# A list scheduler's later landings, its margin at projection matmuls and its cost of wide GpSimd additions, in a one-core encoder trunk

## Chip, cores and metric

The kernel runs on one core of one Trainium2 chip. The metric is the device time of one execution in microseconds; lower is better. Five engines work beside each other, each through its own instructions in a fixed order: TensorE (PE, with its weight loads shown as PEld), VectorE (DVE), ScalarE (ACT), GpSimd (POOL) and SyncE (SP), which issues the DMA transfers. An instruction that waits for a semaphore holds up all that stand behind it on its engine.

## The reference

One layer of an encoder trunk on 2048 prompt tokens and 32 sample tokens, model width 1024, all in float32. Each stream goes through a mixer and a feed-forward part, both with a shift, scale and gate that come from a conditioning vector:

```
p = h @ w_in                                   # 1024 -> 3080 columns
uv, qkv, z, ab = p[..., :o1], p[..., o1:o2], p[..., o2:o3], p[..., o3:]
a_out = spatial_gating(u, v, sgu_w, sgu_b)     # u, v = split(gelu(uv)), chunks of 128 positions
qkv, new_buf = causal_conv(qkv, conv_buf, conv_w)
o, s_new = gated_delta_rule(q, k, vv, beta, g, s0)   # 4 heads x 128, a state carried from chunk to chunk
out = jnp.concatenate([a_out, b_out], axis=-1) @ w_out
x = x + gt1 * m
h = rmsnorm(x, norm_ffn_g[l]) * (1 + sc2) + sh2
x = x + gt2 * (jnp.square(jax.nn.relu(h @ w_up[l])) @ w_down[l])   # 1024 -> 4096 -> 1024
```

A final RMSNorm follows. The outputs are the tokens of both streams and the states.

## The kernel before

Activations lie transposed, channels on the 128 partitions and tokens in the columns. Every large product is made of three matmuls on split operands: a value is cast to a rounded high part (on ACT), and the rest is the low part (a subtraction on DVE, in some places on POOL), and the product is high x high + low x high + high x low (`mm3`, and `split`, `operand`, `slab` for the operands). So each weight block that is loaded (in pieces of 256 or 512 KB) passes through ACT and then DVE before PE may use it.

The work comes in three stages. After a short start, `mixers` goes over two halves of the tokens: the projections of `w_in` column by column (`gemm`, in PSUM banks called g), the delta rule of four heads (`delta_local` and `delta_inv` within chunks, `delta_chain` over the chunks, in banks L, B and C), the spatial gating, and then the output projection. The delta chain hands a small product from PE to DVE or ACT and back several times a chunk; projection matmuls fill the time between. Last comes `feed_forward`, in four blocks of 520 tokens: `ffn_up` and `ffn_down` form their products from seven instead of eight block products each (sums and differences of the weights' and values' blocks), in single PSUM banks f that are taken and given back. In the first block the weights' sums are formed on POOL and stored for later blocks; later blocks load them again (`su_d`, `sd_d`). In `ffn_up`, bank X takes a product, DVE adds it to another value (`u2`, `v5`), and the bank then accumulates a further product, which therefore waits until DVE has read the bank.

The order of all this is not written by hand. Each operation is recorded with its engine, a cost in nanoseconds, what it reads and writes, and a priority: CHAIN, INV, LOCAL, EVAC, GEMM from first to last; the projections' matmuls alone have GEMM (`at(GEMM)` around `mm3`), and among those and the evacuations the one that is due first goes first. `Program.schedule` (L237) then plays the five engines and one DMA engine forward in time by those costs: an operation is ready when all before it have ended, plus a table's latency between the two engines (`LATENCY`), and each engine takes the ready operation of the first priority. A load occupies the planned DMA engine for its bytes / 360 ns, at least 500, and lands `DMA_LATENCY` later (a little sooner for small ones). The outcome is only an order for each engine; at run time the semaphores decide when each instruction starts. A planned time that is too short thus puts an instruction too early in its engine's line, and one that is too long puts it too late. `tt` (L343) sets the cost of an elementwise operation of two tensors; on POOL 150 ns and 2.1 ns a column, for narrow multiplications 1.65.

Of the kernel before, what the change touches and what calls it, by code (L numbers as in the profile page):

```python
# [11 lines left out]
ALU = mybir.AluOpType  # L12
# [28 lines left out]
PE, DVE, ACT, POOL, DMA, NONE = range(6)  # L41
TABLES = {AF.Silu: "silu", AF.Gelu_apprx_tanh: "gelu", AF.Exp: "exp", AF.Ln: "ln"}

DMA_LATENCY = 3000


LATENCY = {(PE, DVE): 230, (PE, ACT): 230, (PE, POOL): 230, (DVE, PE): 380, (DVE, DVE): 130, (DVE, ACT): 160,
           (DVE, POOL): 190, (DVE, DMA): 150, (ACT, PE): 370, (ACT, DVE): 175, (ACT, ACT): 180, (ACT, POOL): 210,
           (ACT, DMA): 150, (POOL, PE): 390, (POOL, DVE): 100, (POOL, ACT): 130, (POOL, POOL): 130, (POOL, DMA): 100}
# [5 lines left out]
CHAIN, INV, LOCAL, EVAC, GEMM, IDLE = range(6)  # L55
# [133 lines left out]
def R(x):  # L189
    return x.ap if isinstance(x, View) else x  # L190
# [10 lines left out]
class Program:  # L201
# [35 lines left out]
    def schedule(self):  # L237

        ops = self.ops
        due = [i if o.eng == PE and o.prio == GEMM else len(ops) for i, o in enumerate(ops)]  # L240
        for i in reversed(range(len(ops))):
            due[i] = min([due[i]] + [due[j] for j in ops[i].succ])
        key = [(o.prio, due[i] if o.prio >= EVAC else i, i) for i, o in enumerate(ops)]
        free = [0.0] * 6
        port = [0.0] * 6
        wait = [[] for _ in range(6)]
        ready = [([], []) for _ in range(6)]
        table, grid = None, (P, P)
        order = []

        def release(i, t):
            o = ops[i]
            if o.eng == NONE:
                finish(i, t, t)
            else:
                heapq.heappush(wait[o.eng], (t, i))

        def finish(i, start, end):
            o = ops[i]
            o.start = start  # L260
            order.append((start, i))
            for j in o.succ:
                s = ops[j]
                s.ready = max(s.ready, end + o.lat + LATENCY.get((o.eng, s.eng), 0.0))
                s.npred -= 1
                if s.npred == 0:
                    release(j, s.ready)

        for i, o in enumerate(ops):
            if o.npred == 0 and o.start == 0.0 and o.eng != NONE:  # L270
                heapq.heappush(wait[o.eng], (0.0, i))
        for i, o in enumerate(ops):
            if o.npred == 0 and o.eng == NONE and not any(k == i for _, k in order[-1:]):
                finish(i, 0.0, 0.0)
                o.npred = -1

        other = {DVE: POOL, POOL: DVE}
        while True:
            best = None
            for e in range(5):  # L280
                shared = port[other[e]] - PORT if e in other else 0.0
                t = None
                if ready[e][0]:
                    t = free[e]
                elif ready[e][1]:
                    t = max(free[e], shared)
                if wait[e]:
                    at, i = wait[e][0]
                    at = max(free[e], at, shared if ops[i].port else 0.0)
                    t = at if t is None else min(t, at)  # L290
                if t is not None and (best is None or t < best[0]):
                    best = (t, e)
            if best is None:
                break
            t, e = best
            while wait[e] and wait[e][0][0] <= t:
                i = heapq.heappop(wait[e])[1]
                heapq.heappush(ready[e][ops[i].port], key[i])
            shared = port[other[e]] - PORT if e in other else 0.0
            tops = [q for q in (ready[e][0], ready[e][1] if shared <= t else None) if q]  # L300
            if not tops:
                continue
            i = heapq.heappop(min(tops, key=lambda q: q[0]))[-1]
            o = ops[i]
            end = t + o.cost
            if e == PE:
                if o.table and o.table != grid:
                    end += 195 if o.table == (P, P) else 135
                    grid = o.table
            elif o.table and o.table != table:  # L310
                end += 1280
                table = o.table
            free[e] = end
            if o.port:
                port[e] = end
            finish(i, t, end)
        assert len(order) == len(ops), (len(order), len(ops))
        self.span = max(free)
        order.sort()
        return [ops[i] for _, i in order]  # L320


class Kern:
# [19 lines left out]
    def tt(self, out, a, b, op, eng=DVE):  # L343
        n = out.n
        if eng == DVE:
            c = 68 + 1.042 * n
        elif op == ALU.pow:
            c = 300 + 165 * n
        else:
            c = 150 + (1.65 if op == ALU.mult and n < 300 else 2.1) * n  # L350
        e = self._e(eng)
        self.p.op(eng, c, lambda: e.tensor_tensor(out=R(out), in0=R(a), in1=R(b), op=op), [out], [a, b])  # L352

# [31 lines left out]
    def dma(self, out, in_, n=None):  # L385
# [3 lines left out]
        x = b / 360  # L389
        self.p.op(DMA, max(500, x), lambda: nc.sync.dma_start(out=R(out), in_=R(in_)), [out], [in_], lat=DMA_LATENCY + min(0, x - 500))  # L390

# [1470 lines left out]
```

## Time and profile before

| what | value |
|---|---|
| time, median of 3 runs | 2437.33 us (2435.55 to 2437.97) |
| profiled execution, first to last instruction | 2450.8 us |
| mean granted clock of TensorE | 0.989 |
| DMA moved | 574.85 MB, 235 GB/s on average |

The runs are timed without the profiler, the profile is of one further execution; its span is 13.5 us above the median. No other time of the profiled execution is given. Busy times are read from the page's first part and from the busy times by stretch; "f<-s" is what an instruction writes and reads, by the program's names without buffer numbers, L398 the line of the matmul helper and L337, L352 and L357 those of ACT's and DVE's helpers, so groups are told apart by tiles and shapes. A bracket such as [2.02 <-DVE s L352] is the engine's idle time before an instruction and what ended it.

### The profile page before, as it was taken

The page shows a single profiled execution, that of the slowest core. Times are in us where ns is not written, and L with a number is a line of the kernel's source. Part 1 is how long each engine was busy: PE and PEld are TensorE (multiplying, and loading weights), DVE is VectorE, ACT ScalarE, POOL GpSimd, SP SyncE. Part 2 cuts the span into 40 slices and gives each one's busy share as a digit, 9 for nine tenths or more (in the row PEclk, how much of TensorE's full clock was granted, in tenths as well). Part 3 has the DMA queues.
Part 4 walks back from the last instruction along what each step waited for, and adds up shares of the span by engine and source line. Part 5 has one row for each costly group of instructions (what it writes and reads, how often), then busy time and mean ns, then how long its engine had stood idle before and what let it go on. Part 6 is the DMA issues. An engine that isn't in the chain of part 4 may idle for free.

```text
span 2450.8 us, 53625 instructions
## 1 busy us (share of the span) xinstructions
PE 2372.3 (97%) x18786; PEld 2217.0 (90%) x18786; DVE 1749.2 (71%) x4041; ACT 1563.5 (64%) x3727; POOL 790.0 (32%) x1079
## 2 busy tenths in 40 slices
PE   7998999999999999999999999999899999899998
PEld 4876878999999878999999999999899999899998
DVE  5555666556665546488677778889788888877786
ACT  4454656455565435375455687777788877887774
POOL 2134422202432223455333453333721213511111
PEclk9999999999999899999999999999999999999999
DMA  8688667555457767888667787888788877787773
GB/s 305 206 298 264 211 199 243 143 180 161 145 181 215 239 183 231 269 273 275 240 215 244 251 265 242 268 273 275 240 266 289 267 256 231 248 279 220 246 232 117
DMA packets 389687, 574.85 MB, mean 235 GB/s; under 512 B 71628, under 2 KB 201568, under 8 KB 389416
## 3 DMA queue, kind: packets, MB, share of 16 engines
q1 hardware_dynamic: 389416, 571.42, 72.2%
q8 instruction: 148, 2.42, 0.4%
q14 instruction: 123, 1.01, 0.1%
HBM read 434.80 MB, written 136.45 MB: 233 GB/s over the span
## 4 chain that ended last, share of the span: by engine, by line
PE 27%; DVE 9%; DMA 8%; ACT 5%; issue 2%; POOL 1%; SPq 0%; DVEq 0%; ACTq 0%; POOLq 0%
PE f L398 27%; DVE s L352 6%; DMA s<-su_d 3%; ACT s L337 2%; DVE s L357 1%; ACT wh L337 1%; DMA s<-w_u 1%; DMA wr<-su_d 1%; DVE wl L352 1%; DVE BL L352 1%; ACT wl L337 1%; DMA wr<-w_u 1%; POOL s L352 1%; DMA s<-sd_d 1%; DMA s<-th_d 0%
## 5 line engine op out<-in xcount | busy, mean ns | idle before, releaser
L337 ACT ACTIVATE s<-s 128x260 f32<-128x260 f32 (+11 forms) x1398 | 611.5, 464 | 338.8 <-DVE s L357 99.5
L398 PE MATMUL f<-s,s 128*128 128x260 f32 x3984 | 538.5, 284 | 8.2 <-ACT s L337 3.6
L352 POOL TENSOR_TENSOR s<-s,s 128x260 f32<-128x260 f32 (+3 forms) x369 | 374.3, 1027 | 518.1 <-ACT s L337 377.0
L398 PE MATMUL f<-BH,wh 128*128 128x260 f32 x1800 | 514.0, 286 | 13.4 <-DVE s L352 9.1
L398 PE MATMUL f<-BH,wl 128*128 128x260 f32 x1800 | 511.1, 284 | 3.6 <-DVE wl L352 2.6
L398 PEld LDWEIGHTS f<-s,s 128*128 128x128 f32 x3984 | 501.8, 189 | 13.6 <-DVE s L352 6.3
L398 PE MATMUL f<-BL,wh 128*128 128x260 f32 x1800 | 509.9, 283 | 1.9 <-DVE BL L352 1.9
L352 DVE TENSOR_TENSOR s<-s,s 128x260 fp32r<-128x260 f32 (+5 forms) x740 | 413.4, 576 | 71.3 <-ACT s L337 43.6
L398 PE MATMUL g<-BH,wh 128*128 128x512 f32 (+2 forms) x1112 | 424.7, 382 | 0.0
L352 DVE TENSOR_TENSOR s<-f,s 128x260 f32<-128x260 f32 x856 | 345.6, 420 | 94.6 <-PE f L398 91.4
L398 PE MATMUL g<-BH,wl 128*128 128x512 f32 (+2 forms) x1112 | 395.0, 355 | 0.0
L398 PE MATMUL g<-BL,wh 128*128 128x512 f32 (+2 forms) x1112 | 393.8, 354 | 0.6 <-DVE BL L352 0.6
L398 PEld LDWEIGHTS f<-BH,wh 128*128 128x128 f32 x1800 | 340.4, 189 | 18.1 <-DVE s L352 6.7
L398 PEld LDWEIGHTS f<-BH,wl 128*128 128x128 f32 x1800 | 341.0, 189 | 5.1 <-DVE wl L352 3.7
L398 PEld LDWEIGHTS f<-BL,wh 128*128 128x128 f32 x1800 | 341.1, 190 | 2.8 <-DVE BL L352 2.7
L352 POOL TENSOR_TENSOR s<-s 128x260 f32<-128x260 f32 (+11 forms) x321 | 167.3, 521 | 531.8 <-DVE s L352 264.1
L337 ACT ACTIVATE wh<-s 128x512 fp32r<-128x512 f32 (+1 forms) x364 | 228.0, 630 | 83.8 <-DMA s<-w_u 25.2
L398 PE MATMUL f<-BH,s 128*128 128x260 f32 x1040 | 240.0, 285 | 0.9 <-ACT BH L337 0.6
L398 PEld LDWEIGHTS g<-BH,wh 128*128 128x128 f32 x1112 | 212.4, 191 | 24.7 <-issue 8.5
L398 PEld LDWEIGHTS g<-BH,wl 128*128 128x128 f32 x1112 | 211.9, 191 | 19.6
L398 PEld LDWEIGHTS g<-BL,wh 128*128 128x128 f32 x1112 | 213.2, 192 | 15.2 <-DVE BL L352 1.1
L357 DVE SCALAR_TENSOR_TENSOR s<-s,s,s 128x512 f32<-128x512 f32 (+6 forms) x318 | 165.0, 535 | 70.5 <-ACT s L337 40.5
(119 smaller groups left out, 3566.4 us busy)
## 6 DMA issues: line engine op xcount, KB each, us to landing
s<-su_d SPq DMA_DIRECT2D x288, 256.0 KB, 4.2
s<-w_u SPq DMA_DIRECT2D x168, 256.0 KB, 4.1
s<-w_d SPq DMA_DIRECT2D x150, 256.0 KB, 4.5
s<-sd_d SPq DMA_DIRECT2D x115, 256.0 KB, 4.0
wr<-su_d SPq DMA_DIRECT2D x96, 256.0 KB, 3.9
wr<-w_b SPq DMA_DIRECT2D x42, 512.0 KB, 5.6
wr<-w_d SPq DMA_DIRECT2D x68, 256.0 KB, 4.7
s<-x_d SPq DMA_DIRECT2D x128, 130.0 KB, 3.6
```

Source lines behind the costliest of these rows:

```text
L337: self.p.op(ACT, c, lambda: nc.scalar.activation(out=R(out), in_=R(in_), func=func, **{k: R(v) for k, v in kw.items()}), [out, accum], [in ...
L352: self.p.op(eng, c, lambda: e.tensor_tensor(out=R(out), in0=R(a), in1=R(b), op=op), [out], [a, b])
L357: self.p.op(DVE, c, lambda: nc.vector.scalar_tensor_tensor(out=R(out), in0=R(a), scalar=R(s), in1=R(b), op0=op0, op1=op1), [out], [a, s, b])
L398: nc.tensor.matmul(R(out), R(l), R(r), **kw)
```

## The change

Three numbers of the planner change; no instruction is added or taken out. A load is planned to land 500 ns later (`DMA_LATENCY` 3500). A GEMM matmul on PE counts as ready 400 ns later than before (`SPARE`) whenever the operation that it waits for ran on another engine or was a load; other priorities and PE's own products get no margin. And a two-tensor operation on POOL of 400 columns or more costs 2.35 instead of 2.1 ns a column in the plan.

```diff
-DMA_LATENCY = 3000
+DMA_LATENCY = 3500
+
+
+SPARE = 400
...
             for j in o.succ:
                 s = ops[j]
-                s.ready = max(s.ready, end + o.lat + LATENCY.get((o.eng, s.eng), 0.0))
+                spare = SPARE if s.eng == PE and s.prio == GEMM and o.eng != PE else 0.0
+                s.ready = max(s.ready, end + o.lat + LATENCY.get((o.eng, s.eng), 0.0) + spare)
...
         else:
-            c = 150 + (1.65 if op == ALU.mult and n < 300 else 2.1) * n
+            c = 150 + (1.65 if op == ALU.mult and n < 300 else 2.1 if n < 400 else 2.35) * n
```

What it moves is seen in the orders of the engines. Line numbers are four larger after the change, and numbers behind a tile's name are buffers.

First DVE, in the second feed-forward block (the place at 1552 to 1556 us of the trace). f4, f5 and f7 are PSUM banks of `ffn_up`; s3 with s10, and wl with wh, are low and high parts of weights whose raw values s0 and s1 are loads; `s22<-f5,s16` is the addition `v5` that reads bank X. Before:

```order
L352 TENSOR_TENSOR s9_9960<-s21_426,s8_10756 128x512
L352 TENSOR_TENSOR s9_9960<-s0_405,s8_10756 128x512
L352 TENSOR_TENSOR s16_421<-f4_18046,s16_421 128x260
L352 TENSOR_TENSOR s3_9853<-s1_406,s10_10019 128x512
L352 TENSOR_TENSOR wl_11725<-s1_406,wh_11724 128x512
L352 TENSOR_TENSOR s22_427<-f5_18111,s16_421 128x260
```

And now:

```order
L356 TENSOR_TENSOR s9_10039<-s21_426,s8_10890 128x512
L356 TENSOR_TENSOR s16_421<-f4_18080,s16_421 128x260
L356 TENSOR_TENSOR s9_10039<-s0_405,s8_10890 128x512
L356 TENSOR_TENSOR s22_427<-f5_18131,s16_421 128x260
L356 TENSOR_TENSOR s3_9931<-s1_406,s10_10085 128x512
L356 TENSOR_TENSOR s7_412<-s6_411,s7_412 128x260
L356 TENSOR_TENSOR wl_11723<-s1_406,wh_11722 128x512
```

The addition that reads bank f5 stood behind the two splits of weights from s1 and now stands ahead of both.

Second ACT, in the first feed-forward block (1159 to 1170 us of the trace). wh are high parts of `ffn_up`'s weights, whose raw values in s2 here are sums that POOL formed; s23 holds values on their way through relu and square, and s17 high parts of those. Before:

```order
L337 ACTIVATE wh_11724<-s2_407 128x512
L337 ACTIVATE wh_11726<-s2_407 128x512
L337 ACTIVATE wh_11726<-s0_405 128x512
L337 ACTIVATE wh_11726<-s2_407 128x512
L337 ACTIVATE s23_428<-s23_428 128x260 x2
L337 ACTIVATE wh_11726<-s0_405 128x512
L337 ACTIVATE s17_10806<-s23_428 128x260
L337 ACTIVATE s23_428<-s23_428 128x260
```

And now:

```order
L341 ACTIVATE wh_11724<-s0_405 128x512
L341 ACTIVATE s23_428<-s23_428 128x260 x2
L341 ACTIVATE wh_11724<-s0_405 128x512
L341 ACTIVATE s17_10909<-s23_428 128x260
L341 ACTIVATE wh_11724<-s2_407 128x512
L341 ACTIVATE s23_428<-f6_12958 128x260
```

The last of the casts from s2 stood ahead of two operations of s23, a cast from s0 and one into s17; these four now stand ahead of it.

Third PE, in the third block (1924 us of the trace). f6 takes `ffn_up`'s fourth product; f7 is bank X, which DVE must have read before it accumulates the fifth; f5 is bank W of the sixth, whose reader, a copy of the first product, was done long before. Before:

```order
L398 MATMUL f6_23119<-BH1_72,wh_11724 128x260
L398 MATMUL f6_23119<-BL1_80,wh_11724 128x260
L398 MATMUL f6_23119<-BH1_72,wl_11725 128x260
L398 MATMUL f7_23088<-BH6_77,wh_11726 128x260
L398 MATMUL f7_23088<-BL6_85,wh_11726 128x260
L398 MATMUL f7_23088<-BH6_77,wl_11727 128x260
```

And now:

```order
L402 MATMUL f6_23143<-BH1_72,wh_11722 128x260
L402 MATMUL f6_23143<-BL1_80,wh_11722 128x260
L402 MATMUL f6_23143<-BH1_72,wl_11723 128x260
L402 MATMUL f5_23000<-BH2_73,wh_11724 128x260
L402 MATMUL f5_23000<-BL2_81,wh_11724 128x260
L402 MATMUL f5_23000<-BH2_73,wl_11725 128x260
L402 MATMUL f7_23137<-BH6_77,wh_11724 128x260
```

The first three matmuls of the sixth product, which came behind all twelve of the fifth, now stand ahead of it.

## The prediction

> **What bounds the kernel now.** I read the page's first part, then the busy times by stretch, then the waits of TensorE (PE), and last the timeline at the longest of those waits.
>
> ```profile
> span 2450.8 us, 53625 instructions
> PE 2372.3 (97%) x18786; PEld 2217.0 (90%) x18786; DVE 1749.2 (71%) x4041; ACT 1563.5 (64%) x3727; POOL 790.0 (32%) x1079
> ```
>
> PE is the bound: it is idle for 2450.8 - 2372.3 = 78.5 us of the span. The diff neither adds nor removes an instruction, so nothing beyond those 78.5 us, and what stalls do to PE's clock, can be won. The stretches are the start, the mixers with the output projection, and the feed-forward:
>
> ```profile
> 0.00:66.00 66.00, 49.03 (x298) 29.92 (x299) 36.97 (x87) 31.32 (x50) 17.82 (x24) 1.00 0.86 296
> 66.00:1066.00 1000.00, 977.82 (x7519) 860.28 (x7518) 591.14 (x1620) 528.68 (x1388) 309.83 (x593) 0.99 0.68 211
> 1066.00:2450.00 1384.00, 1345.48 (x10975) 1326.85 (x10973) 1121.06 (x2336) 1003.47 (x2290) 462.39 (x462) 0.99 0.76 249
> ```
>
> The first number behind the comma is PE's busy time, so it idles 17.0 us in the start, 22.2 us in the mixers and 38.5 us in the feed-forward, where DVE (third number) is busy 1121.06 of 1384 us, 81%: a late DVE has little slack there. PE's waits in that last stretch, by what ended them (total us, times, longest):
>
> ```profile
> PE f L398 <- DVE s L352: 12.4, 20, 2.0
> PE f L398 <- ACT s L337: 4.0, 6, 1.9
> PE f L398 <- ACT BH L337: 3.7, 3, 1.7
> PE f L398 <- DVE BL L352: 3.5, 9, 1.2
> PE f L398 <- DVE wl L352: 2.3, 3, 1.0
> PE M L409 <- POOL rcol L352: 1.6, 2, 1.0
> ```
>
> These six sum to 27.5 us, and none is on a load directly. Where they come from is seen at the longest of them:
>
> ```profile
> 1553.31 0.63 ACT L337 ACTIVATE s<-s 128x512 fp32r<-128x512 f32 x1 [2.33 <-DMA s<-w_d]
> 1552.08 0.42 DVE L352 TENSOR_TENSOR s<-f,s 128x260 f32<-128x260 f32 x1
> 1553.97 0.69 DVE L352 TENSOR_TENSOR s<-s,s 128x512 fp32r<-128x512 f32 x1 [1.47 <-ACT s L337]
> 1554.60 0.69 DVE L352 TENSOR_TENSOR wl<-s,wh 128x512 fp32r<-128x512 f32 x1
> 1555.20 0.42 DVE L352 TENSOR_TENSOR s<-f,s 128x260 f32<-128x260 f32 x1
> 1555.68 0.39 PE L398 MATMUL f<-BH,wh 128*128 128x260 f32 x1 [2.02 <-DVE s L352]
> ```
>
> ACT's next cast in line stood 2.33 us for a load of w_d that landed later than planned; DVE's split of the same weights stood 1.47 us behind the cast; behind the two splits in DVE's order stood the addition that reads PSUM (1555.20), and PE could not accumulate into that bank before it: 2.02 us lost. So the mechanism is head-of-line blocking: the plan put an operation that was not ready ahead of one that was.
>
> **The change, part by part.** 1. *Later landings.* The planner lets a load of 256 KB (728 ns on its DMA engine) land 3.73 us after its start, of 512 KB 4.46 us, of 128 KB 3.36 us; now each 0.5 us later. Measured, from issue to landing (KB each, median us):
>
> ```profile
> s<-su_d SPq DMA_DIRECT2D x288, 256.0 KB, 4.2
> s<-w_d SPq DMA_DIRECT2D x150, 256.0 KB, 4.5
> wr<-w_b SPq DMA_DIRECT2D x42, 512.0 KB, 5.6
> s<-z_d SPq DMA_DIRECT2D x32, 128.0 KB, 2.2
> ```
>
> For the weights the new plan (4.23 and 4.96 us) is nearer to what happens, though still short of it; for the z rows it moves further off. 2. *Wide GpSimd additions.* 512 columns were planned at 1225 ns and are now at 1353, 400 columns at 1090 after 990:
>
> ```profile
> L352 POOL TENSOR_TENSOR s<-s,s 128x512 f32<-128x512 f32 x83 | 121.3, 1464 | 112.1 <-ACT s L337 60.1 <-DVE wl L352 29.3 <-ACT wh L337 11.8
> L352 POOL TENSOR_TENSOR s<-s,s 128x400 f32<-128x400 f32 x32 | 37.6, 1176 | 43.9 <-ACT s L337 36.8 <-issue 6.4
> ```
>
> With 1464 and 1176 ns measured, this also goes half way towards the chip. It decides most in the first feed-forward block, which sums its weights on POOL:
>
> ```profile
> 1167.44 0.63 ACT L337 ACTIVATE wh<-s 128x512 fp32r<-128x512 f32 x1 [4.38 <-POOL s L352]
> 1167.98 0.86 ACT L337 ACTIVATE s<-s 128x260 f32<-128x260 f32 x2
> 1168.75 0.62 ACT L337 ACTIVATE wh<-s 128x512 fp32r<-128x512 f32 x1
> 1169.27 0.71 ACT L337 ACTIVATE s<-s 128x260 fp32r<-128x260 f32 x2
> 1171.54 0.38 PE L398 MATMUL f<-s,s 128*128 128x260 f32 x1 [1.89 <-ACT s L337]
> ```
>
> 3. *The margin.* A projection's matmul whose operand or bank comes from another engine counts as ready 400 ns later, so PE's order puts three more matmuls of another product ahead of it. At eight places in the feed-forward the bank's reader on DVE comes too late by 0.2 to 0.6 us, one of them:
>
> ```profile
> 1924.85 0.36 PE L398 MATMUL f<-BH,wh 128*128 128x260 f32 x1 [0.38 <-DVE s L352]
> ```
>
> **The sum,** against the profiled execution. (a) I traced each PE wait of the feed-forward above 0.06 us back along the engine that ended it. In 21 of them, 11.4 us counting the late start of the matmul behind, the instruction that blocked the line stands behind the needed one in the new order. The first two shown above are among them, and a third, behind a load of w_u:
>
> ```profile
> 2056.46 0.69 DVE L352 TENSOR_TENSOR wl<-wr,wh 128x512 fp32r<-128x512 f32 x1 [1.54 <-ACT wh L337]
> 2059.09 0.48 PE L398 MATMUL f<-s,s 128*128 128x260 f32 x2 [0.74 <-DVE s L357]
> ```
>
> At 1555 DVE's addition no longer stands behind the two splits: after the one of 1552.08 it can end by some 1552.08 + 0.42 + 0.42 = 1552.9, and PE asked for the bank at 1555.68 - 2.02 = 1553.66, so 2.02 us are gone. At 1171 four of the five ACT operations of 1167.98 to 1169.98 now run inside the 4.38 us of waiting, 1.6 us of work; one of 0.3 us comes in between, so some 1.3 of 1.89 us go. At 2059 DVE's addition passes the split: 0.6 of 0.74. Together 3.9 us. Of the other 18 (6.3 us) I take half, since what is late next is usually the following DVE operation: 3.1. Bounds of (a): 3.9 and 11.4; I take 7.0. (b) The margin, eight places of three matmuls. An undisturbed stretch gives a matmul's pace:
>
> ```profile
> 1200.00:1300.00 100.00, 100.00 (x836) 100.00 (x836) 67.36 (x128) 49.10 (x107) 42.10 (x31) 1.00 0.62 215
> 1173.20:1176.60 3.40, 3.40 (x18) 3.40 (x17) 2.33 (x4) 2.40 (x5) 0.00 (x0) 0.50 1.02 362
> ```
>
> 100 us / 836 = 0.12 us, so 0.36 us of cover each, of which 0.3 is needed: 2.4 us, between 0 and 2.9. (c) The second row is what follows the wait at 1171: 3.4 us at a granted clock of 0.50, 18 matmuls instead of 28, some 1.4 us lost. Five such windows lie in the feed-forward; I count one away, 1.4 us, bounds 0 and 7. The Trainium skill's page "TensorE: Matmul & The Clock Gate", section "Part 1: The HAM clock gate", has the clock halve after at least one idle window of about 3.4 us; by that rule no wait here, all of them under 2.1 us, could cost clock, and the sum would lack this term: 2430.7 us in place of 2429.3. The row above disagrees, since PE was idle for only 1.89 us before it. (d) New waits: where the blocks of the feed-forward meet (near 1745 and 2132 us) some products of ffn_down lose up to 3.6 us of the matmuls that stood between their bank's reader and them; I charge 2.8 us, bounds 0 and 6.
>
> (e) The mixers: 0. Counted over the whole order, 49 of the delta chain's 323 hand-overs from PE through DVE or ACT and back have more projection matmuls between them than before (31.6 us in all) and 53 fewer (33.3 us). The two cancel; a third of the 22.2 us of idle time either way, 7 us, is my bound. (f) Moved DMA issues: the loads keep one SP queue, whose instructions wait in line for their buffers,
>
> ```profile
> SPq L390 <- DVE s L352: 355.9, 421, 9.2
> ```
>
> 421 times and 0.85 us on average; a load that falls behind one more of these lands about that much later. Weights are loaded some microseconds ahead, so I take 0, and as bounds two such delays either way, -2 and +2. Start and end keep their order where PE waits: 0. Sum: 7.0 + 2.4 + 1.4 - 2.8 = 8.0 us of 2450.8. The profiled span lies 13.5 us above the median of 2437.33, and the stalls should be the same in both, so I subtract from the median: 2429.3 us, **2429**.
>
> **The rivals.** *The waits are traded.* DVE is busy 81% of the feed-forward and works in line; what passes a blocked split delays that split, and its product waits instead. For it: six groups of PE waits have six different enders, no single one. Against: the split at 1555 was not needed by the next product at all. Then (a) is worth its lower bound, (d) takes it all: 2437.3 - 3.9 - 2.4 + 6 = 2437. The same time comes out if loads land before the plan, as the z rows do (2.2 against 3.36 us): then their users only move back. The Trainium skill's page "DMA: Bandwidth & Descriptors", section "Anatomy of one DMA — SWDGE (gpsimd) path", fits 2.0 us plus the bytes over 436 GB/s for loads that GpSimd issues, an estimate of 2.6 us for 256 KB, by which even the old plan was late enough; the rows of 4.2 and 4.5 us speak against it for these loads on SP.
>
> *Slower: the chain runs bare.* The margin delays the plan's filler, not the delta chain, so the chain's step may be planned next although a filler was ready. A filler triple of 512 columns is 3 x 0.12 x 512/260 = 0.7 us. If 25 of the 53 hand-overs that lost filler become waits of 0.7 us, and the 49 others gain nothing, the mixers lose 17.5 us: 2429.3 + 17.5 = 2447; from 19 of them on (13 us) the whole is slower by over 0.2%. For it: these hand-overs have little reserve. Against: PE's waits for the chain (tile C) are few now, and the counts cancel.
>
> *More is won:* all of (a) and (b), four clock windows of (c), no (d): 2437.3 - 11.4 - 2.9 - 5.6 = 2417.
>
> **How the numbers follow.** Forecast 2429: 0.46. Traded, 2437: 0.28, of which 0.04 for loads before the plan. Chain bare, 2447: 0.17. More, 2417: 0.09. A measurement of this kernel can tell about 0.2%, 4.9 us, from no change. Faster by more: 0.46 + 0.09 = 0.55; within it 0.28; slower 0.17. The range takes the forecast with its mixers' bound of 7 us, most of the larger gain, and the near half of the slower case: 2416 to 2444.
>
> **What would show it.** At the places of 1555, 1171 and 2059 us PE's waits should be under 0.7 us; "PE f <- DVE s" in the feed-forward should fall from 12.4 to about 7 us, and PE's idle time there from 38.5 to about 31 us; at most four windows of half clock should lie there; the mixers should keep 22 us, give or take 7. I am wrong if ACT still waits for w_d and w_u at the head of its line before a PSUM reader, or if waits of tile C grow to over 10 us.

## The result and the profile after

| | before | after |
|---|---|---|
| time, median | 2437.65 us (2435.55 to 2447.0) | 2410.43 us (2405.68 to 2414.47) |
| ratio, 95% interval | 1 | 0.9889 [0.9859, 0.9919] |
| profiled execution, first to last instruction | 2450.8 us | 2412.6 us |
| mean granted clock of TensorE | 0.989 | 0.995 |

The change makes the kernel 27 us faster, 1.1%. The forecast was 2429 us, its range 2416 to 2444: the direction was right, the size was not. The first part of the page after:

```profile
span 2412.6 us, 53571 instructions
...
PE 2346.5 (97%) x18786; PEld 2203.2 (91%) x18786; DVE 1739.8 (72%) x4041; ACT 1558.5 (65%) x3727; POOL 774.0 (32%) x1079
```

The span is 38.2 us shorter, but PE's idle time only fell from 78.5 to 2412.6 - 2346.5 = 66.1 us. The other 25.8 us came out of what is counted as busy, with the same 18786 matmuls.

The feed-forward's first matmul (the first that writes a bank f) starts at 1054.1 us before the change and at 1034.0 us after it. Cut there, the stretches are (PE, PEld, DVE, ACT, POOL busy, then the granted clock), before,

```profile
66.00:1054.10 988.10, 966.82 (x7434) 849.90 (x7432) 579.78 (x1599) 521.74 (x1371) 304.84 (x589) 0.99 0.67 211
1054.10:2450.00 1395.90, 1356.48 (x11059) 1337.22 (x11058) 1132.43 (x2358) 1010.41 (x2306) 467.39 (x466) 0.99 0.76 249
```

and after, with the start and the stretch from 1066 us on besides:

```profile
0.00:66.00 66.00, 46.41 (x297) 28.74 (x298) 37.53 (x87) 31.46 (x50) 18.34 (x24) 1.00 0.89 303
66.00:1034.00 968.00, 954.98 (x7434) 842.34 (x7433) 576.24 (x1601) 519.58 (x1370) 297.28 (x590) 1.00 0.68 214
1034.00:2412.00 1378.00, 1345.10 (x11059) 1332.11 (x11058) 1126.00 (x2356) 1007.48 (x2308) 458.40 (x466) 0.99 0.77 252
1066.00:2412.00 1346.00, 1315.72 (x10831) 1304.19 (x10829) 1097.71 (x2310) 983.99 (x2250) 440.42 (x453) 0.99 0.77 251
```

PE idles 13.0 us after 21.3 in the mixers with the output projection, and 32.9 after 39.4 in the feed-forward. The mixers' 20 us flatter the change, though, since the profiled execution of the kernel before was a long one. neutral_shift, the kernel before with loads planned to land at 3010 instead of 3000 ns, takes as long as the kernel before (below). Its first feed-forward matmul and that of the change (the numbers ahead of "to" are the first start):

```profile
L398 PE MATMUL f<-BH,wh x1800: 277/283/480, 1041.0 to 2427.1; 128*128 128x260 f32 x180
L402 PE MATMUL f<-BH,wh x1800: 277/283/584, 1034.0 to 2401.2; 128*128 128x260 f32 x180
```

Against this kernel, with a span of 2438.8 us, the change reaches the feed-forward 7.0 us sooner and needs 1378.6 instead of 1397.8 us from there on: 19.2 us of the gain lie in the feed-forward. PE's waits there from 1066 us on, by what ended them (us in total, times, longest):

```profile
PE f L402 <- DVE s L356: 10.0, 11, 3.9
PE f L402 <- DVE BL L356: 7.0, 7, 2.3
PE M L413 <- POOL rcol L356: 2.3, 3, 1.0
PE f L402 <- DVE wl L356: 1.2, 1, 1.2
...
PE f L402 <- ACT BH L341: 0.6, 2, 0.4
PE f L402 <- ACT s L341: 0.6, 2, 0.5
```

Those that ACT ended are nearly gone (4.0 and 3.7 us before). Those that DVE ended on s are fewer, 10.0 us after 12.4, and BL grew from 3.5 to 7.0. The place that was at 1555 us lies at 1529 us now:

```profile
1527.24 0.63 ACT L341 ACTIVATE s<-s 128x512 fp32r<-128x512 f32 x1 [2.26 <-DMA s<-w_d]
...
1527.91 0.69 DVE L356 TENSOR_TENSOR s<-s,s 128x512 fp32r<-128x512 f32 x1 [1.59 <-ACT s L341]
...
1528.52 0.42 DVE L356 TENSOR_TENSOR s<-f,s 128x260 f32<-128x260 f32 x1
...
1528.99 0.39 PE L402 MATMUL f<-BH,wh 128*128 128x260 f32 x1 [0.67 <-DVE s L356]
```

The load of w_d is as late for ACT as before (2.26 after 2.33 us), and DVE's split waits as long (1.59 after 1.47). But one split now stands ahead of the addition that PE needs, not two, and PE loses 0.67 instead of 2.02 us. At this place head-of-line blocking is relieved by the order, not by a faster load.

**A measure that holds across kernels.** A matmul of 260 columns is shown for 0.28 us though the next one follows 0.12 us later, so a gap of up to 0.16 us is hidden in busy time. I therefore summed from the trace every gap over 0.06 us between the starts of two successive matmuls beyond the first one's pace (0.12 us at 260 columns, 0.23 at 512), and apart from those what matmuls lost inside stretches at half clock. The start is left out. Each row is one execution. The base is neutral_shift, since its profiled span, 2438.8 us, is an ordinary one.

| kernel | gaps: mixers | output projection | feed-forward | at half clock | sum against neutral_shift | medians' difference |
|---|---|---|---|---|---|---|
| before (long execution) | 87.8 | 7.7 | 57.5 | 21.8 | +10.2 | |
| neutral_shift | 81.9 | 10.3 | 60.3 | 12.1 | 0 | 0 |
| after | 78.2 | 8.8 | 43.2 | 7.8 | -26.6 | -27.1 |
| landing_2500 | 93.8 | 13.2 | 82.6 | 8.5 | +33.5 | +38.0 |
| landing_only | 75.0 | 9.2 | 40.5 | 6.2 | -33.7 | -33.0 |
| landing_4000 | 76.8 | 6.6 | 37.4 | 24.3 | -19.5 | -22.1 |
| landing_in_ffn | 84.4 | 7.7 | 39.1 | 5.1 | -28.3 | -23.8 |
| landing_in_mixers | 74.0 | 8.5 | 53.9 | 8.1 | -20.1 | -19.2 |
| landing_and_pool | 71.0 | 5.6 | 40.2 | 5.2 | -42.6 | -44.3 |
| margin_in_mixers | 77.5 | 7.0 | 38.8 | 11.1 | -30.2 | -33.3 |
| change_3510 | 76.1 | 7.0 | 34.4 | 2.9 | -44.2 | -46.7 |

Where a median stands beside the sum, the two agree within 5 us, so the table shows in which stage the time of these executions went.

### The profile page after: what moved, and what is told of

Read it like the earlier page. It is cut to its first block, busy times and chain, and to the rows that moved or that the text cites. A ratio compares the mean times of both kernels' runs of the same rounds, so it can differ in the third digit from the quotient of the medians.

```text
span 2412.6 us, 53571 instructions
## 1 busy us (share of the span) xinstructions
PE 2346.5 (97%) x18786; PEld 2203.2 (91%) x18786; DVE 1739.8 (72%) x4041; ACT 1558.5 (65%) x3727; POOL 774.0 (32%) x1079
## 4 chain that ended last, share of the span: by engine, by line
PE 75%; DVE 8%; DMA 6%; ACT 5%; issue 4%; POOL 1%; SPq 0%; DVEq 0%; POOLq 0%; ACTq 0%
PE f L402 40%; PE g L402 26%; DVE s L356 4%; PE C L402 3%; ACT s L341 3%; PE B L402 2%; DVE s L361 2%; DMA s<-su_d 1%; PE L L402 1%; DVE BL L356 1%; ACT wh L341 1%; DVE wl L356 1%; PE M L402 1%; PE L L413 1%; POOL s L356 1%
## 5 line engine op out<-in xcount | busy, mean ns | idle before, releaser
L341 ACT ACTIVATE s<-s 128x260 f32<-128x260 f32 (+10 forms) x1398 | 612.7, 465 | 340.8 <-DVE s L361 98.9
L356 POOL TENSOR_TENSOR s<-s,s 128x260 f32<-128x260 f32 (+3 forms) x369 | 368.4, 1009 | 504.3 <-ACT s L341 383.9
L356 DVE TENSOR_TENSOR s<-s,s 128x512 fp32r<-128x512 f32 (+5 forms) x740 | 412.5, 575 | 51.0 <-ACT s L341 34.0
L402 PEld LDWEIGHTS g<-BH,wh 128*128 128x128 f32 x1112 | 210.9, 190 | 25.8 <-issue 7.2
L402 PEld LDWEIGHTS g<-BH,wl 128*128 128x128 f32 x1112 | 210.2, 189 | 19.2
L361 DVE SCALAR_TENSOR_TENSOR s<-s,s,s 128x400 f32<-128x400 f32 (+5 forms) x318 | 162.5, 526 | 67.8 <-ACT s L341 40.9
```

The costliest lines, as they stand in the source:

```text
L341: self.p.op(ACT, c, lambda: nc.scalar.activation(out=R(out), in_=R(in_), func=func, **{k: R(v) for k, v in kw.items()}), [out, accum], [in ...
L361: self.p.op(DVE, c, lambda: nc.vector.scalar_tensor_tensor(out=R(out), in0=R(a), scalar=R(s), in1=R(b), op0=op0, op1=op1), [out], [a, s, b])
L402: nc.tensor.matmul(R(out), R(l), R(r), **kw)
```

## The experiments

Theories: **A**, the three edits each give a share and add up. **B**, the margin carries the gain. **C**, it is luck: any change of the plan's numbers reshuffles the order. **D**, the later landing carries it, since loads that are planned too early block the lines of ACT and DVE everywhere. The kernel before took 2438 to 2440 us in the median of each comparison (single times 2430 to 2451).

**Each edit alone, and an edit without meaning.** landing_only:

```diff
-DMA_LATENCY = 3000
+DMA_LATENCY = 3500
```

> Loads planned 500 ns later, no margin, POOL cost as before. Theory A (each of the three numbers brings the plan nearer to the chip, and their gains add to about 27 us): 2425 to 2431, about a third of the gain or a little more. Theory B (the margin carries nearly all): 2435 to 2440, no change. Theory C (any reshuffle moves the time by some 10 us either way, and the change had luck): anywhere from 2422 to 2450, and no better than the neutral shift.

2404.51 us, ratio 0.9859 [0.9829, 0.9889]: all of the change's gain and 6 us more. margin_only:

```diff
+SPARE = 400
...
-                s.ready = max(s.ready, end + o.lat + LATENCY.get((o.eng, s.eng), 0.0))
+                spare = SPARE if s.eng == PE and s.prio == GEMM and o.eng != PE else 0.0
+                s.ready = max(s.ready, end + o.lat + LATENCY.get((o.eng, s.eng), 0.0) + spare)
```

> The 400 ns margin at the projections' matmuls alone. Theory A: 2424 to 2431. Theory B: 2408 to 2418, nearly the whole gain, with PE's waits in the mixers and in the feed-forward both down by half of what the whole change took or more. Theory C: anywhere from 2422 to 2450.

2428.86 us, 0.995 [0.9931, 0.997]. pool_only:

```diff
-            c = 150 + (1.65 if op == ALU.mult and n < 300 else 2.1) * n
+            c = 150 + (1.65 if op == ALU.mult and n < 300 else 2.1 if n < 400 else 2.35) * n
```

> Wide POOL additions at 2.35 ns a column alone. Theory A: 2430 to 2435, with the wait of 1.9 us in the first feed-forward block gone. Theory B: 2435 to 2440. Theory C: 2422 to 2450.

2430.92 us, 0.9966 [0.9948, 0.9984]. neutral_shift:

```diff
-DMA_LATENCY = 3000
+DMA_LATENCY = 3010
```

> The kernel before with loads planned 10 ns later, 3010 instead of 3000: it reorders about half of the rows of DVE and ACT and a quarter of PE's, without bringing the plan nearer to the chip in any way that counts. Theories A and B: 2434 to 2441, within 0.2% of the kernel before. Theory C: off by 5 to 15 us either way.

2437.52 us, 0.9988 [0.9971, 1.0005]: no difference. 34 + 10 + 8 = 52 us of single gains against 27 us together: A falls. The margin alone gives 10: B falls. C looks weak here, but comes back below.

**The landing's dose.** landing_2500 and landing_4000, nothing else changed:

```diff
-DMA_LATENCY = 3000
+DMA_LATENCY = 2500
```

> The kernel before with loads planned 500 ns earlier, at 2500. Theory D (the planned landing carries the gain, because users of loads then stand where the data has come): the opposite of landing_only, 2455 to 2475, with ACT's waits for loads up. Theory C (a lucky order): 2430 to 2445, no trend.

```diff
-DMA_LATENCY = 3000
+DMA_LATENCY = 4000
```

> The kernel before with loads planned at 4000, so 4.73 us for 256 KB against measured medians of 4.1 to 4.5 us. Theory D: at or a little below landing_only, 2395 to 2405, since late loads above the median are covered too. If only the median counts: 2403 to 2410, no further gain. Theory C: anywhere from 2405 to 2440.

2475.49 us, 1.0157 [1.0122, 1.0193], and 2415.42 us, 0.9896 [0.9864, 0.9927]. ACT's waits for loads show the mechanism; two groups of them, the loads of stored weight sums (us in total, times, longest), with the landing planned at 2500 ns,

```profile
ACT wh L337 <- DMA s<-su_d: 32.4, 38, 2.4
...
ACT wl L337 <- DMA s<-su_d: 24.4, 34, 2.2
```

at 3000, the kernel before,

```profile
ACT wh L337 <- DMA s<-su_d: 21.6, 32, 2.2
...
ACT wl L337 <- DMA s<-su_d: 18.0, 26, 2.1
```

at 3500, landing_only,

```profile
ACT wl L341 <- DMA s<-su_d: 10.1, 14, 1.9
...
ACT wh L341 <- DMA s<-su_d: 6.7, 13, 1.1
```

and at 4000:

```profile
ACT wh L337 <- DMA s<-su_d: 7.1, 13, 1.0
...
ACT wl L337 <- DMA s<-su_d: 5.6, 10, 1.4
```

56.8, 39.6, 16.8 and 12.7 us; all of ACT's waits that a DMA ended sum to 248, 197, 130 and 99 us. Each half microsecond of later landing takes ACT's waits down, and PE's gaps in the feed-forward go with them (82.6, 57.5, 40.5, 37.4 us). D holds there. At 4000 the gaps still shrink, yet the time lies above D's 2395 to 2405 us, since 24.3 us go to half clock in the profiled execution; the granted clock of its four executions is 0.987 to 0.993, that of landing_only's 0.995 to 0.997. The end of the mixers there (granted clock third from the right):

```profile
932.40:939.20 6.80, 6.31 (x21) 5.84 (x22) 4.16 (x9) 2.54 (x5) 1.86 (x3) 0.50 0.52 170
949.50:959.70 10.20, 4.64 (x15) 3.82 (x16) 7.23 (x16) 3.98 (x9) 4.88 (x5) 0.50 0.86 265
```

**Pairs.** landing_and_pool is the change without the margin, landing_and_margin is it without the GpSimd cost, margin_and_pool without the later landing:

```diff
-SPARE = 400
+SPARE = 0
```

> The change without the margin: loads at 3500 and wide POOL additions at 2.35. If the margin is what gives back the 6 us between the whole change and landing_only: 2398 to 2405. If the POOL cost is: 2409 to 2413.

```diff
-            c = 150 + (1.65 if op == ALU.mult and n < 300 else 2.1 if n < 400 else 2.35) * n
+            c = 150 + (1.65 if op == ALU.mult and n < 300 else 2.1) * n
```

> The change without the POOL cost: loads at 3500 and the margin of 400. If the margin is what gives back the 6 us: 2409 to 2416. If the POOL cost is: 2398 to 2405.

```diff
-DMA_LATENCY = 3500
+DMA_LATENCY = 3000
```

> The margin and the GpSimd cost without the later landings. If the two gains seen alone (10 and 8 us) add up: 2439 - 18 = 2421 us. If each only moves a few waits that the other moves too: 2429 us, as one alone. If, as on top of the later landings, the margin costs where the GpSimd cost is right: 2435 us or more.

2393.21 us, 0.9812 [0.9787, 0.9836]; 2403.61 us, 0.9851 [0.9826, 0.9876]; 2429.48 us, 0.9955 [0.9933, 0.9978]. Of the kernels so far, every one with a landing of 3500 ns stands at 2393 to 2410 us, every one with 3000 or 3010 ns at 2428.9 us or more. landing_and_pool beats both kernels: taking the margin out of the change wins 17 us. Without the GpSimd cost the margin takes nothing (2403.61 with it, 2404.51 without).

**Where the landing gains.** One landing up to the output projection, another in the feed-forward; landing_in_ffn, and landing_in_mixers with False and True exchanged:

```diff
-DMA_LATENCY = 3000
+DMA_LATENCY = 3500
...
-        self.p.op(DMA, max(500, x), lambda: nc.sync.dma_start(out=R(out), in_=R(in_)), [out], [in_], lat=DMA_LATENCY + min(0, x - 500))
+        self.p.op(DMA, max(500, x), lambda: nc.sync.dma_start(out=R(out), in_=R(in_)), [out], [in_], lat=(DMA_LATENCY if self.late else 3000) + min(0, x - 500))
...
+            self.late = False
             self.setup()
...
+            self.late = True
             self.feed_forward()
```

> Loads planned to land 3.5 us after their start in the feed-forward alone, 3.0 us before it; no margin, old GpSimd cost. The prediction put the whole gain into the feed-forward and the mixers at 0. By that theory this kernel has all of what landing_only won: 2439 - 34 = about 2405 us, and PE's idle time before the feed-forward is as in the kernel before. By the theory that late loads block ACT's and DVE's lines everywhere, it wins only the feed-forward's part: from the PE gaps that I added up in the trace of landing_only (57.5 to 40.5 us in the feed-forward, 87.8 to 75.0 in the mixers), about 17 to 20 us, so 2419 to 2422 us.

> The complement: 3.5 us from the start to the output projection, 3.0 us in the feed-forward. By the prediction (mixers 0): 2439 us, no difference. By the theory that late loads block the lines everywhere: 13 to 17 us less, 2422 to 2426 us, with the progress of the mixers' matmuls about 15 us ahead of before's where the feed-forward begins. The gains of this kernel and of landing_in_ffn should add up to the 34 us of landing_only within some 6 us.

2413.74 us, 0.9901 [0.9869, 0.9934], and 2418.34 us, 0.9914 [0.9885, 0.9944]: 26 and 21 us, more together (47) than landing_only's 34, so the sum within 6 us that was expected failed. The first feed-forward matmul of the two, in this order:

```profile
L398 PE MATMUL f<-BH,wh x1800: 277/283/420, 1040.5 to 2400.7; 128*128 128x260 f32 x180
L398 PE MATMUL f<-BH,wh x1800: 277/283/548, 1025.0 to 2404.5; 128*128 128x260 f32 x180
```

Against the 1041.0 us of neutral_shift, the later landing in the mixers brings it 16.0 us forward, that in the feed-forward 0.5. The gaps agree: each kernel takes mainly its own stage down (84.4 and 39.1; 74.0 and 53.9 us, against 81.9 and 60.3). Both also shed half clock, 7.0 and 4.0 us, while landing_only sheds 5.9 in all; and landing_in_mixers has 6.4 us less of gaps in the feed-forward too, which no run explains. The mixers gain, then, but less than the feed-forward, which landing_in_ffn shortens by 26.2 us (2412.1 - 1040.5 against 1397.8). In the feed-forward the path is seen: from 1066 to 2400 us ACT waits 61.2 us for loads in landing_in_ffn and 123.4 in landing_in_mixers. From 66 to 1040 us it is 49.1 and 51.1 us, no difference, so how the later landing helps the mixers stays open.

**Where the margin costs.** The margin given to one stage, with all else as in the change; margin_in_mixers has `<` for `>=`, and margin_mixers_800 besides `SPARE = 800`:

```diff
-                spare = SPARE if s.eng == PE and s.prio == GEMM and o.eng != PE else 0.0
+                spare = SPARE if s.eng == PE and s.prio == GEMM and o.eng != PE and j >= self.late else 0.0
...
+            self.p.late = len(self.p.ops)
             self.feed_forward()
```

> The changed kernel with the margin given to the matmuls of the feed-forward alone; later landings and the GpSimd cost as in the change. landing_and_pool, without any margin, took 2393 us, the change 2410 us. If the margin costs in the mixers (it delays projection matmuls that fill the delta chain's gaps; PE's gaps there were 71.0 us without it and 78.2 us with it, in the feed-forward 40.2 and 43.2 us), this kernel takes 2393 to 2398 us. If it costs in the feed-forward, 2405 to 2410 us. If the margin does good in the feed-forward, as the prediction had it (2.4 us), 2391 us.

> The changed kernel with the margin given to the matmuls ahead of the feed-forward alone. If the margin costs its 17 us in the mixers: 2408 to 2412 us, as the change. If the cost appeared only with both together: 2393 to 2398 us.

> The margin doubled to 800 ns, in the matmuls ahead of the feed-forward alone. If a margin delays the filler of the delta chain, a larger one costs more: 2420 us or above. If the 17 us are the scatter of a reshuffled plan, it may come out anywhere between 2393 and 2410 us, or below.

2393.86 us, 0.9812 [0.978, 0.9843]; 2404.2 us, 0.9854 [0.9834, 0.9874]; 2405.98 us, 0.9862 [0.9843, 0.9881]. In these plans the margin neither gives nor takes in the feed-forward (2393.21 without it); in the mixers it costs 11 us, and hardly more when doubled. One place where it is lost is the end of the delta chain, in the timeline of the change:

```profile
951.68 0.24 PE L413 MATMUL C<-ident,s 32*128 32x32 f32 x1 [1.61 <-DVE s L370]
...
952.33 0.40 SPq L394 DMA_DIRECT2D mix_d<-s  x1
952.74 0.54 ACT L341 ACTIVATE BH<-s 128x400 fp32r<-128x400 f32 x1 [2.25 <-DMA s<-mix_d]
...
953.33 0.45 PE L402 MATMUL g<-BH,wh 128*128 128x400 f32 x1 [1.40 <-ACT BH L341]
...
954.59 0.45 PE L402 MATMUL g<-BL,wh 128*128 128x400 f32 x1 [0.80 <-DVE BL L356]
```

and in that of landing_and_pool:

```profile
933.10 0.34 PE L402 MATMUL g<-BH,wl 128*128 128x400 f32 x1
933.38 0.24 PE L413 MATMUL C<-ident,s 32*128 32x32 f32 x1
933.55 0.45 PE L402 MATMUL g<-BH,wh 128*128 128x400 f32 x1
```

In the second the chain's last step comes while PE still has matmuls of the output projection, and more follow at once. In the change those are used up: PE stands for the chain, then for the rows that pass through mix_d, then for their split, 3.81 us in all, and a stretch of half clock follows:

```profile
955.10:958.50 3.40, 3.40 (x16) 3.13 (x15) 1.56 (x4) 2.70 (x6) 2.38 (x3) 0.50 0.88 271
```

**Is it the margin, or that order?** Shifts of 10 ns around landing_and_pool and around the change itself:

```diff
-DMA_LATENCY = 3500
+DMA_LATENCY = 3490
```

> landing_and_pool with a load planned 10 ns earlier, no margin: no mechanism, only another tie-break in the plan. If the scatter of plans is small: 2390 to 2397 us. If scatter explains the margin's 17 us: this or its twin at 3510 is off by 8 us or more.

> The twin, 10 ns later, no margin. The same two expectations: 2390 to 2397 us if plans near to each other take about the same time; off by 8 us or more if the scatter of plans is as large as the margin's cost.

> The change with the landing planned 10 ns earlier. If the margin by its nature leaves the chain bare at its end: 2404 to 2412 us, with PE waits of some 3.8 us at the last step of the delta chain, as in the change. If the change's order was only unlucky: 2391 to 2399 us, as landing_3490_and_pool, without those waits.

> The twin, 10 ns later. The same two expectations: 2404 to 2412 us with the waits at the chain's last step if the margin causes them, 2391 to 2399 us without them if the order was unlucky.

Without the margin 2397.04 us, 0.983 [0.9807, 0.9853], and 2395.9 us, 0.9824 [0.9803, 0.9846]. With it 2399.5 us, 0.9857 [0.9831, 0.9883], and 2390.87 us, 0.9807 [0.9789, 0.9826]. At the chain's last step in the two changed kernels:

```profile
945.21 0.24 PE L413 MATMUL C<-ident,s 32*128 32x32 f32 x1
```

(3490) and

```profile
941.85 0.24 PE L413 MATMUL C<-ident,s 32*128 32x32 f32 x1
```

(3510), no wait. So the end of the chain standing bare isn't what a margin must do; it belongs to the order that came out at exactly these numbers. landing_4000, which has no margin, stands 3.05 us at the same step. Ten nanoseconds away the same three edits take 11 and 20 us less: C was right about most of the margin's cost, though not about the gain. Three neighbours without the margin lie at 2393, 2396 and 2397 us, three with it at 2391, 2400 and 2410. What the margin does by itself is not shown; a small cost in the mixers is likely, since the feed-forward begins at 1018.4 to 1020.5 us in the four plans with the later landing, the GpSimd cost and no margin there, and at 1023.0 to 1034.0 in the five with one. Nor is it shown for the GpSimd cost: its 8 us alone, and the 11 between landing_only and landing_and_pool, are differences of single plans.

## Why the prediction was half right

- **The mechanism**, loads landing after their planned time and so putting casts and splits at the head of ACT's and DVE's lines, was right for the feed-forward; the dose and landing_in_ffn show it. The three places that the prediction named do not. PE's wait fell there from 2.02 to 0.67, from 1.89 to 0 and from 0.74 to 0 us, all under the 0.7 us that it asked for. But at the same matmuls neutral_shift, which gains nothing, has 0, 1.93 and 0 us: a new order alone clears single waits and makes others. And a sign of being wrong did show, ACT's 2.26 us for w_d at the head of its line, only with one split fewer behind it. (For the loads of su_d the new plan of 4.23 us was not short of the measured 4.2, as the prediction had it of all weights.)
- **Two steps failed, first the size of (a), the feed-forward's waits, 7.0 us.** The whole 8.0 us of the forecast lay in the feed-forward, and the change took 19.2 us out of it against neutral_shift. The gaps there fell by 17.1 us (60.3 to 43.2; by 14.3 from the long execution's 57.5), more than the 11.4 us that bound (a) from above. Two things were mis-sized. The sum was made of waits that the profile shows as idle time, while a good part of the gaps is hidden under the matmuls' modelled ends: of the 25.8 us that came out of busy time 14.0 are half clock (21.8 to 7.8), a loss that the prediction allowed for, and some 8 of the other 11.8 are such gaps, which it did not: the gaps fell by 22.8 us, the idle time behind the start by 14.8. And half of the 18 untested places was taken for "what is late next", but with later landings the next one is late less often too. The idle time forecast there, 31 us, came out (30.3 from 1066 us on); "PE f <- DVE s" fell to 10.0, not to 7.
- **(e), the mixers at 0, is the second.** landing_in_mixers begins the feed-forward 16.0 us sooner than neutral_shift (9.7 of it gaps), outside the bound of 7; the change, whose order gave part of it back, 7.0 us (5.2 of it gaps). The step counted only which hand-overs of the chain gained or lost filler on PE, and let those cancel. It did not ask what the landing does to the projections in between. Its bound was a third of 22.2 us of idle time, while the gaps between matmuls sum to 87.8 us in the mixers.
- **(b), the margin, 2.4 us**: not shown. The wait at 1924 us is gone, but also in landing_only, pool_only and neutral_shift, with no margin.
- **(c), the clock, 1.4 us**: its own row gives (28 - 18) x 0.12 = 1.2 us a window. Three windows of half clock lie in the feed-forward after the change (at most four were forecast), five before. In the whole kernel, the end apart, ten windows became five. Against neutral_shift the gain is 12.1 - 7.8 = 4.3 us, but in one execution each; the granted clock of the kernel before ran from 0.989 to 0.995 between executions.
- **(d), new waits where the blocks meet, 2.8 us, came out in size and not in kind.** PE's waits around the two boundaries were 6.2 + 6.6 us and are 9.0 + 6.8: 3.0 us more. The step had in mind readers of a bank that lose the matmuls which covered them. But the two longest waits, 2.30 us at 1747 and 3.89 at 2088, each stand behind one DVE instruction that took 4.54 and 5.00 us (the medians of their shapes are 0.42 and 0.68) while POOL ran additions beside it, which the prediction did not foresee; that the sizes meet is luck. Here the first:

```profile
1742.60 4.54 DVE L356 TENSOR_TENSOR BL<-s,BH 128x260 fp32r<-128x260 f32 x1 [0.43 <-ACT BH L341]
1744.04 2.81 POOL L356 TENSOR_TENSOR s<-s,s 128x260 f32<-128x260 f32 x4
1747.19 0.58 PE L402 MATMUL f<-BL,wh 128*128 128x260 f32 x1 [2.30 <-DVE BL L356]
```

- **The base.** The prediction took the 13.5 us between span and median to be no part of the stalls. After, the profiled execution's own time is known, 2414.47 us for a span of 2412.6. With the same 1.9 us around it, the one before took some 2452.7 us, an estimate, and above every timed one. What it had more of was half clock, 21.8 us against the 12.1 of neutral_shift; one of its stretches:

```profile
811.40:821.60 10.20, 10.20 (x60) 9.45 (x61) 3.56 (x12) 2.10 (x5) 4.79 (x16) 0.50 0.68 211
```

- **The rivals.** "The chain runs bare" happened, but at two places instead of 25, and the waits of tile C did not grow to 10 us (5.6 before, 5.8 after): at the chain's end (3.81 us and a window of half clock), and near the middle of the mixers, where the change lost 5.4 us more between 440 and 520 us than landing_and_pool did. The order at 3500 ns takes 11 and 20 us more than its two neighbours'. "More is won" was right in its direction; it, too, looked only at the feed-forward. (f), the moved DMA issues, was not tested by itself.

## What to carry to other kernels

When a list scheduler's planned latency is short of the measured one, correct it first, and try a value on either side: the dose told the mechanism from luck. Single waits that vanish do not: a plan that gained nothing cleared two of the three named here. A scheduler's output scatters: here 10 ns in one constant moved the time by up to 20 us, so judge a margin or a tie-break by several neighbouring plans, and ship the best of them (2391 us here) rather than the first. And measure the stalls of an engine full of short matmuls from start to start, since the idle time showed only a third of this gain.

## What the runs showed of the hardware

**Half clock after short waits.** In the change, PE waits 1.80 us at 486.2 us, and from 487.4 us on:

```profile
487.40:490.80 3.40, 3.40 (x18) 3.40 (x18) 0.31 (x2) 2.07 (x6) 0.00 (x0) 0.51 0.64 224
```

The lengths seen, the end apart, are 3.4, 6.8 and 10.2 us, and once 13.7 (landing_2500). The Trainium skill's page "TensorE: Matmul & The Clock Gate", section "Part 1: The HAM clock gate", asks for at least one idle window of about 3.4 us first; of the three windows in the change's feed-forward one does follow a wait that long (3.89 us), the others waits of 1.45 and 0.81 us, and of 2.30 us. Here shorter waits are enough.

What decides can be worked out from the twenty traces. In each of them the stretches of half clock start and end on a grid of 3.413 us (within 0.03 us), whose offset differs from execution to execution. Cut each feed-forward, from 1060 us to 20 us before the end, into the cells of its own grid, and call a cell filled as far as the paces of its matmuls (0.12 us at 260 columns) cover it. All 49 stretches of half clock there follow a cell filled to 0.414 or less, 48 of them to 0.40 or less. Of the 7714 other cells at full clock one is that empty (0.39); the next has 0.417. So a cell filled to less than some 40% brings half clock in the next one: the 1.89 us at 1171 us before the change left its cell filled to 0.35, and half clock followed; the 2.02 us at 1555 left 0.42, and none did. Where a wait falls on the grid is thus luck, and may be part of why executions of one kernel differ.

**DVE beside POOL.** In the change's feed-forward 16 DVE instructions took over 1 us more than the median of their form. All 16 ran beside a POOL instruction for 0.69 or more of their time, while POOL is busy for a third of the span. The two longest (4.54 and 5.00 us, beside POOL for 0.98 and 0.93) made PE's two longest waits there. Why most meetings of the two engines cost less was not tested.

**A pause with no releaser.** At 486 us of the change, ahead of the half clock shown above, PE stood in the middle of a run of small matmuls without a wait that the trace shows:

```profile
486.19 0.30 PE L402 MATMUL B<-s,s 32*32 32x16 f32 x12 [1.80 <-issue]
```

The kernel before has one of 1.5 us on the same tile, margin_mixers_800 one of 2.77 us. Its cause was not looked into.
